# A two-layer trunk on one core: eight feature tiles of each down-projection as seven block products, and V in sixteen parts shifted by a token tile

## The chip, the core and the metric

The kernel runs on one core of a Trainium2 chip. Its parts are TensorE (PE in the profile; it multiplies, into the accumulators of PSUM), VectorE (DVE) and ScalarE (ACT), which read and write PSUM and the on-chip memory, GpSimd (POOL), and the DMA queues, of which SyncE (SP) and GpSimd issue the transfers here. Each engine runs its instructions strictly in the order in which the program has them; an instruction that waits holds everything behind it on its engine. The metric is the device time of one execution in microseconds (us); lower is better.

## The reference

One batch of 512 tokens, width 1024, float32. Layer 0 mixes tokens with differential attention (8 heads, block-causal mask), layer 1 with a gated short convolution. Each is followed by a SwiGLU channel mixer, and each of the four sublayers sits in `x <- LN(alpha * x + sublayer(x))`:

```python
def swiglu(x, w_gate, w_up, w_down):          # D_FF = 2816 = 22 feature tiles of 128
    h = jax.nn.silu(x @ w_gate) * (x @ w_up)
    return h @ w_down
...
for i in range(2):
    m = diff_attention(h, ...) if i == 0 else short_gated_conv(h, ...)
    h = layer_norm(ALPHA * h + m, ln1_g[i], ln1_b[i])
    h = layer_norm(ALPHA * h + swiglu(h, w_gate[i], w_up[i], w_down[i]), ln2_g[i], ln2_b[i])
```

## The kernel before, in words

**Numbers.** Every operand of a large product is split in two rounded parts, hi = round(x) and lo = x - hi, and a product is three matmuls: hi·hi, hi·lo, lo·hi (`mm3`). `split` makes the pair: ScalarE copies hi, VectorE subtracts for lo. Where a weight is used unchanged in gate/up, `plain` makes the pair in another way: ScalarE copies hi, ScalarE copies -hi into lo, and a GpSimd DMA adds the raw weight to lo in place (the accumulate).

**Stages.** Attention (to about 196 us of the profiled execution), the output projection, gate/up of layer 0 (246 to 466), its down-projection (466 to 590), the convolution (590 to 771), gate/up of layer 1 (to 990) and its down-projection (to the end).

**Attention.** For each head h, `project_qk(h)` multiplies q and k in 8 parts and `project_v(h // 2, h % 2)` half of the token tiles of V for a pair of heads in 4 parts: two tiles share a PSUM bank, and one ScalarE copy per bank puts them into `v_sb`. Between these 12 parts, at set places, stand the steps of the head before, `attend(h - 1)`: scores, transposes of the map, and the products with V (`values`, one per query tile `qt`, which reads the tiles 0 to `qt` of `v_sb`).

**Gate/up** is by seven block products (Winograd's form of Strassen's scheme: x11, s2, s1, x12, s3, s4, x22) over 11 units of two feature tiles. The hidden activations of a unit go to a tile `h{u}`, two feature tiles by 512 tokens. The forms of the input lie in slots `f0` to `f13`, named by `HOME`.

**Down-projection** (`project_norm` with name `dn`): 22 feature tiles in 11 groups of two; the output is two halves of 512 columns by four token tiles. For each half, each weight group (one 512 KB load, one `split`) is multiplied with the hidden pairs `hid` of the four token tiles, into one bank per token tile (`o_dn`). Before it, `swiglu` splits the 11 hidden tiles, partly into the slots of the forms. After each half, `residual` adds the bank to `ALPHA *` the residual `res`, and the norm follows.

**Order.** The program has no loop on the chip. A scheduling layer lays the instructions out once, engine by engine, from the order of the code and its own priorities; buffers of a pool rotate, and a load or a write waits until the last reader of its buffer is done.

Of the kernel before, what the change touches and what calls it, by code (L numbers as in the profile page):

```python
# [34 lines left out]
UNITS = KF // 2  # L35
LEAD = 4
# [3 lines left out]
def trunk(ctx: ExitStack, tc: tile.TileContext, t: dict):  # L40
# [208 lines left out]
    def project_norm(lhs, w, kt, gb, xT, out, name, early=None, fetch=None):  # L249
# [10 lines left out]
        def step(ps, wg, gi, j, tt, at=None):  # L260
            k = gi * GROUP + j
            ts = slice(tt * P, (tt + 1) * P)
            n = 512 // len(ps[tt])
            for i in range(len(ps[tt])) if at is None else (at,):
                cs = slice(i * n, (i + 1) * n)
                lh, ll = lhs(k)
                mm3(ps[tt][i][:, :n], (lh[:, ts], ll[:, ts]),
                    (wg[0][:, j, cs], wg[1][:, j, cs]), k == 0, k == kt - 1)

        def residual(ps, hf, tt, i=0):  # L270
            n = 512 // len(ps[tt])
            r = res[:, tt, hf * 512 + i * n : hf * 512 + (i + 1) * n]
            nc.vector.scalar_tensor_tensor(r, r, ALPHA, ps[tt][i][:, :n], op0=ALU.mult, op1=ALU.add)
# [14 lines left out]
        ps = [[bank(f"o_{name}_1_{tt}")] for tt in range(NT)]  # L288
# [33 lines left out]
    with ExitStack() as actx:  # L322
# [111 lines left out]
        def project_v(pair, th):  # L434
            state = {}

            def part(u, half):
                tt = 2 * th + u
                if (u, half) == (0, 0):
                    state["ps"] = bank(f"v_{pair}_{th}")  # L440
                    if pair and th == 0:
# [10 lines left out]
            return [lambda u=u, half=half: part(u, half) for u in range(2) for half in range(2)]  # L452
# [94 lines left out]
        def attend(h):  # L547
# [56 lines left out]
    def swiglu(i, x, turns, open_next, out):  # L604
# [3 lines left out]
        with ExitStack() as fctx:  # L608
# [136 lines left out]
        with ExitStack() as fctx:  # L745
            dx = fctx.enter_context(tc.tile_pool(name=f"dx{i}", bufs=1, reuse_waits="tile"))
            hT = []
            for u in range(UNITS):
                if u == 0:
                    hi = wpool.tile([P, 2, S], F32R, tag="whi", name=f"hid{i}_{u}_hi")  # L750
                    lo = wpool.tile([P, 2, S], F32R, tag="wlo", name=f"hid{i}_{u}_lo")
                elif u < 8:
                    hi, lo = (slot(slots["f"], f"f{2 * u - 2 + j}", (2, S), F32R, f"hid{i}_{u}_{j}") for j in range(2))
                else:
                    hi, lo = (slot(dx, f"d{2 * u + j}", (2, S), F32R, f"hid{i}_{u}_{j}") for j in range(2))
# [125 lines left out]
```

## Time and profile before

| | |
|---|---|
| median of 3 runs (lowest to highest) | 1125.2 us (1124.7 to 1125.24) |
| the profiled execution: its own time, and its span | 1126.72 us, 1124.9 us |
| PE busy | 1105.3 us, 98% of the span |
| VectorE, ScalarE, GpSimd busy | 733.4, 516.8, 115.0 us |
| mean granted clock of PE | 0.997 of full speed |
| bytes moved by DMA | 156.63 MB, mean 139 GB/s |

The span runs from the first to the last instruction that the profiler saw; the execution's own time is 1.8 us longer. Matmuls overlap: the profile gives each its own duration, but the distance between the starts of two that follow each other is what a matmul costs.

### The profile page before, as it was taken

Reading aid. Unit: us, or ns where it says so; the run is one execution under the profiler, and the core shown is the slowest. Engines: PE = TensorE matmul, PEld = TensorE weight load, DVE = VectorE, ACT = ScalarE, POOL = GpSimd, SP = SyncE. Lnnn points to the kernel's source line nnn. Section 1 sums busy time; section 2 is a strip of 40 time slices with the busy share of each in tenths; the row PEclk is TensorE's granted clock in tenths of the full one; section 3 lists DMA queues with packets and bytes.
Section 4 is the critical chain, followed back from the end, with each engine's and each line's share of the span. In section 5 each row is a group of like instructions: output and inputs, shape, how many; then the busy total and the mean of one; then the engine's idle time right before and its main releaser. Section 6 shows DMA issues by size and latency. Waiting matters only on the chain.

```text
span 1124.9 us, 17891 instructions
## 1 busy us (share of the span) xinstructions
PE 1105.3 (98%) x7242; PEld 992.1 (88%) x7242; DVE 733.4 (65%) x1067; ACT 516.8 (46%) x788; POOL 115.0 (10%) x147
## 2 busy tenths in 40 slices
PE   8999999999999999999999999999999999999997
PEld 6878887889999999988889888889999999988886
DVE  7888877588987676924264634448898677672416
ACT  5555555656466566612222323336546556651210
POOL 1111111130011111000010000012001111100002
PEclk9999999999999999999999999999999999999999
DMA  8512132376777875533314433368558777553302
GB/s 276 201 38 76 57 95 75 83 172 200 231 180 205 185 189 133 169 113 92 114 38 137 134 104 95 94 144 214 181 178 205 187 188 180 125 181 94 112 20 75
DMA packets 45027, 156.63 MB, mean 139 GB/s; under 512 B 5232, under 2 KB 6128, under 8 KB 44944
## 3 DMA queue, kind: packets, MB, share of 16 engines
q1 hardware_dynamic: 35728, 121.93, 33.9%
q0 software_dynamic: 9216, 33.56, 16.0%
q8 instruction: 57, 0.93, 0.3%
q14 instruction: 26, 0.21, 0.1%
HBM read 119.81 MB, written 2.10 MB: 108 GB/s over the span
## 4 chain that ended last, share of the span: by engine, by line
PE 85%; DVE 6%; issue 4%; ACT 2%; DMA 2%; POOL 0%; SPq 0%; POOLq 0%; DVEq 0%; ACTq 0%
PE y L636 16%; PE z L636 11%; PE x L636 10%; PE o_dn L75 7%; PE o_dn L76 7%; PE o_dn L74 7%; PE in L74 4%; PE in L76 4%; PE in L75 4%; PE o_wo L74 1%; PE o_wco L74 1%; PE o_wco L76 1%; PE o_wco L75 1%; PE o_wo L76 1%; PE o_wo L75 1%
## 5 line engine op out<-in xcount | busy, mean ns | idle before, releaser
L56 ACT CAST whi_gu_t<-gu_t 128x1024 fp32r<-128x1024 f32 x88 | 89.8, 1049 | 100.5 <-DVE gu_t L624 90.7
L57 DVE TENSOR_TENSOR wlo_dn<-raw_dn,whi_dn 128x1024 fp32r<-128x1024 f32 x44 | 53.3, 1222 | 110.3 <-ACT whi_dn L56 110.3
L74 PE MATMUL o_dn<-whi_dn,hid 128*128 128x512 f32 (+1 forms) x320 | 123.8, 387 | 0.0
L76 PE MATMUL o_dn<-whi_dn,hid 128*128 128x512 f32 (+1 forms) x320 | 123.8, 387 | 0.0
L75 PE MATMUL o_dn<-wlo_dn,hid 128*128 128x512 f32 (+1 forms) x320 | 123.8, 387 | 0.0
L57 DVE TENSOR_TENSOR wlo_gu_t<-gu_t,whi_gu_t 128x1024 fp32r<-128x1024 f32 x88 | 106.3, 1219 | 3.6 <-ACT whi_gu_t L56 3.6
L56 ACT CAST whi_dn<-raw_dn 128x1024 fp32r<-128x1024 f32 x44 | 45.8, 1050 | 135.5 <-PE o_dn L76 106.0
L174 POOL DMA_DIRECT2D wlo_gu<-raw_gu x64 | 55.8, 872 | 432.8 <-ACT wlo_gu L173 377.7
L636 PE MATMUL x<-x_x_hi,whi_gu 128*128 128x256 f32 x352 | 98.6, 280 | 0.0
L636 PE MATMUL x<-x_x_hi,wlo_gu 128*128 128x256 f32 x352 | 98.4, 280 | 0.0
L636 PE MATMUL y<-x_s_hi,wlo_gu_t 128*128 128x256 f32 x352 | 98.3, 279 | 0.0
L636 PE MATMUL y<-x_s_hi,whi_gu_t 128*128 128x256 f32 x352 | 98.3, 279 | 0.0
L636 PE MATMUL x<-x_x_lo,whi_gu 128*128 128x256 f32 x352 | 98.2, 279 | 0.0
L636 PE MATMUL y<-x_s_lo,whi_gu_t 128*128 128x256 f32 x352 | 98.2, 279 | 0.0
L74 PE MATMUL in<-x_hi,whi_in 128*128 128x512 f32 (+1 forms) x240 | 83.7, 349 | 0.0
L76 PE MATMUL in<-x_hi,wlo_in 128*128 128x512 f32 (+1 forms) x240 | 83.2, 347 | 0.0
L75 PE MATMUL in<-x_lo,whi_in 128*128 128x512 f32 (+1 forms) x240 | 82.8, 345 | 0.0
L172 ACT CAST whi_gu<-raw_gu 128x1024 fp32r<-128x1024 f32 x64 | 66.8, 1048 | 30.1 <-PE y L636 21.3
L75 PEld LDWEIGHTS o_dn<-wlo_dn,hid 128*128 128x128 f32 x320 | 60.2, 188 | 13.1
L76 PEld LDWEIGHTS o_dn<-whi_dn,hid 128*128 128x128 f32 x320 | 60.1, 188 | 13.0
L74 PEld LDWEIGHTS o_dn<-whi_dn,hid 128*128 128x128 f32 x320 | 60.2, 188 | 13.0
L173 ACT ACTIVATE wlo_gu<-raw_gu 128x1024 fp32r<-128x1024 f32 x64 | 67.5, 1054 | 7.9 <-PE o_wco L75 6.5
(239 smaller groups left out, 3117.1 us busy)
## 6 DMA issues: line engine op xcount, KB each, us to landing
raw_gu<-in_wgu SPq DMA_DIRECT2D x104, 512.0 KB, 4.6
wlo_gu<-raw_gu POOLq DMA_DIRECT2D x64, 512.0 KB, 5.4
raw_dn<-in_wdn SPq DMA_DIRECT2D x44, 512.0 KB, 3.6
raw_in<-in_win SPq DMA_DIRECT2D x24, 512.0 KB, 3.6
raw_qk<-in_wqk SPq DMA_DIRECT2D x14, 512.0 KB, 3.8
raw_v<-in_wv SPq DMA_DIRECT2D x8, 512.0 KB, 4.8
raw_wo<-in_wo SPq DMA_DIRECT2D x8, 512.0 KB, 3.7
raw_wco<-in_wco SPq DMA_DIRECT2D x8, 512.0 KB, 3.7
```

Of the source, the lines that this page charges most:

```text
L56: nc.scalar.copy(hi, src)
L57: nc.vector.tensor_tensor(lo, src, hi.bitcast(F32), op=ALU.subtract)
L74: nc.tensor.matmul(out, lh, rh, start=first, stop=False)
L75: nc.tensor.matmul(out, lh, rl, start=False, stop=False)
L76: nc.tensor.matmul(out, ll, rh, start=False, stop=last)
L172: nc.scalar.copy(hi, raw)
L173: nc.scalar.activation(lo, raw, AF.Copy, scale=-1.0)
L174: nc.gpsimd.dma_start(lo, raw, accum_op=ALU.add)
L636: nc.tensor.matmul(o, a, b[:, k, :], start=first and f + k + n == 0, stop=k == 3 and n == 2, skip_group_check=True)
```

## The change

In both layers, the feature tiles 0 to 7 of the down-projection (the hidden tiles of units 0 to 3, now one tile `hq`, called `quad`) are multiplied with their 1024 weight rows by seven products of blocks in place of eight. A block is four feature tiles by 256 tokens (`a11`, `a12` of token tiles 0 and 1, even and odd feature tiles; `a21`, `a22` of token tiles 2 and 3), and four feature tiles by 512 columns of the weights (b11, b12, b21, b22; the rows of `wdn` are reordered for this when the inputs are laid out). Each product is 24 matmuls of 512 columns into two banks (x, z or y). Sums of blocks of activations (`v(a11, a11, a21)` and so on, in place) and of weights (t1 to t4) run on VectorE; the sums are split by `split`, the unchanged weight blocks b11, b21 and b22 by `plain`. After a product, VectorE adds its banks to the quarters of `res` that need it, while later products go on accumulating in the same banks. The other 14 feature tiles are multiplied as before, into the banks x, y and z as they stand.

V is projected in sixteen parts, one token tile of a pair of heads each, with a bank and a ScalarE copy of 256 columns each; head 0 has three of them, the heads 1 to 6 two, head 7 one, so that each stands one tile earlier. The products with V stand at the places 6, 7, 9 and 11 for every head.

```diff
 CHUNK = 4
...
     def fetch_gu(i):
         lead[i] = []
+        more = slot(slots["xb"], "hq", (4, 4, 256), F32R, f"wlead{i}")
...
+            pair = (more[:, 2 * u - 4], more[:, 2 * u - 3]) if u >= 2 else None
...
         def residual(ps, hf, tt, i=0):
...
+            if carry is not None and (hf or tt >= 2):
+                nc.vector.tensor_tensor(r, r, ps[tt][i][:, :n], op=ALU.add)
+            else:
+                nc.vector.scalar_tensor_tensor(r, r, ALPHA, ps[tt][i][:, :n], op0=ALU.mult, op1=ALU.add)
...
-        ps = [[bank(f"o_{name}_0_{tt}")] for tt in range(NT)]
+        ps = carry[:4] if carry is not None else [[bank(f"o_{name}_0_{tt}")] for tt in range(NT)]
...
-        def project_v(pair, th):
+        def project_v(pair, tt):
...
-                if (u, half) == (1, 1):
-                    nc.scalar.copy(v_sb[:, 2 * th : 2 * th + 2, pair * 256 : (pair + 1) * 256],
-                                   ps.rearrange("p (t e) -> p t e", t=2))
+                if half == 1:
+                    nc.scalar.copy(v_sb[:, tt, pair * 256 : (pair + 1) * 256], ps[:, :256])
...
-            for qt, i in zip(range(NT), (6, 7, 11, 12) if h % 2 == 0 else (6, 7, 9, 11)):
+            for qt, i in zip(range(NT), (6, 7, 9, 11)):
                 steps[i].append(lambda qt=qt: values(h, qt))
...
             parts = project_qk(h)
-            parts += project_v(h // 2, h % 2)
+            for n in range(2 * h + 1 if h else 0, min(2 * h + 3, 16)):
+                parts += project_v(n // NT, n % NT)
...
+            def load(a, b, g, pool, tag, n):
+                raw = pool.tile([P, 2, 512], F32, tag=tag, name=f"raw_dn{i}_{a}{b}_{g}", bufs=n)
+                nc.sync.dma_start(raw, t["wdn"][i][:, b, CHUNK * a + 2 * g : CHUNK * a + 2 * g + 2, :])
+                return raw
...
+            def plain_dn(raws, name):
+                return [plain(raw, "", pair_dn(f"{name}_{g}")) for g, raw in enumerate(raws)]
+
+            def combined_dn(raws, name):
+                out = []
+                for g, raw in enumerate(raws):
+                    out.append(pair_dn(f"{name}_{g}"))
+                    split(*out[-1], raw)
+                return out
...
+            def product(ps, key, w, first):
+                hi, lo = left[key]
+                for u in range(CHUNK):
+                    wh, wl = w[u // 2]
+                    for j in range(2):
+                        ts = slice(j * P, (j + 1) * P)
+                        mm3(ps[j], (hi[:, u, ts], lo[:, u, ts]), (wh[:, u % 2, :], wl[:, u % 2, :]),
+                            first and u == 0, u == CHUNK - 1, skip_group_check=True)
...
+            banks = {n: [bank(f"{n}_dn{i}_{j}") for j in range(2)] for n in "xzy"}
+            b11 = [load(0, 0, g, wpool, "raw", 3) for g in range(2)]
+            w = plain_dn(b11, "11")
+            form("x11", a11)
+            product(banks["x"], "x11", w, True)
+            b12 = [load(0, 1, g, dx, "b12", 2) for g in range(2)]
+            t1 = sums_dn(b11, b12, b11)
+            form("x12", a12)
+            v(a11, a11, a21, op=ALU.subtract)
+            v(a21, a21, a22, op=ALU.add)
+            form("s1", a21)
+            product(banks["z"], "s1", combined_dn(t1, "t1"), True)
+            for th, half in ((1, 1), (0, 1), (1, 0)):
+                add(th, half, banks["x"], ALPHA)
+            b22 = [load(1, 1, g, dx, "b22", 2) for g in range(2)]
+            t2 = sums_dn([dx.tile([P, 2, 512], F32, tag="t2", name=f"t2_dn{i}_{g}", bufs=2) for g in range(2)], b22, t1)
+            form("x22", a22)
+            v(a22, a22, a11, op=ALU.subtract)
+            form("s2", a22)
+            halve("x11")
+            product(banks["y"], "s2", combined_dn(t2, "t2"), True)
+            add(1, 1, banks["z"])
+            b21 = [load(1, 0, g, dx, "b21", 2) for g in range(2)]
+            halve("s1")
+            product(banks["x"], "x12", plain_dn(b21, "21"), False)
+            add(0, 1, banks["y"])
+            form("s3", a11)
+            halve("s2")
+            t3 = sums_dn(b12, b22, b12)
+            product(banks["y"], "s3", combined_dn(t3, "t3"), False)
+            v(a12, a12, a22, op=ALU.subtract)
+            form("s4", a12)
+            halve("x12")
+            product(banks["z"], "s4", plain_dn(b22, "22"), False)
+            add(1, 1, banks["y"])
+            t4 = sums_dn(t2, b21, t2)
+            halve("s3")
+            product(banks["y"], "x22", combined_dn(t4, "t4"), False)
+            halve("s4")
+            halve("x22")
```

`form(key, src)` splits a block of activations into the slots `HOME[key]`; `halve(key)` splits the hidden tile of the next of units 4 to 10 into the same slots, once the product that read them is done; `add` adds two banks to a quarter of `res` (the three with `ALPHA` by one multiply-and-add).

**How the order of instructions moves.** The rows below are instructions of the built programs in the order of one engine: line, operation, output <- inputs, shape of the output. The lines of the rows after the change are those of the changed kernel, 1 to 110 higher.

The first place is VectorE in layer 0, from the last gate/up unit's `c210_10` on (the first instruction there that reads the last gate/up product). Before the change, the rest of the unit stands between splits of hidden tiles (`hid0_*`) and of weights (`wlo_dn0_*`) for the plain down-projection:

```order
L697 TENSOR_TENSOR c210_10_5521<-e0_10_5329,y0_10_5340 128x512
L57 TENSOR_TENSOR wlo_dn0_0_2_5656<-raw_dn0_0_2_5653,whi_dn0_0_2_5655 128x1024
L57 TENSOR_TENSOR hid0_1_1_5534<-h0_1_3510,hid0_1_0_5533 128x1024
L699 TENSOR_TENSOR h0_10_5490<-c210_10_5521,w50_10_5396 128x2x256
L57 TENSOR_TENSOR wlo_dn0_0_3_5686<-raw_dn0_0_3_5683,whi_dn0_0_3_5685 128x1024
L57 TENSOR_TENSOR wlo_dn0_0_4_5716<-raw_dn0_0_4_5713,whi_dn0_0_4_5715 128x1024
L57 TENSOR_TENSOR hid0_8_1_5562<-h0_8_5022,hid0_8_0_5561 128x1024
```

After the change:

```order
L704 TENSOR_TENSOR c210_10_5531<-e0_10_5339,y0_10_5350 128x512
L58 TENSOR_TENSOR dn0_x22_lo_5650<-hq0_3352,dn0_x22_hi_5649 128x1024
L706 TENSOR_TENSOR h0_10_5500<-c210_10_5531,w50_10_5406 128x2x256
L840 TENSOR_TENSOR hq0_3352<-hq0_3352 128x4x256
L853 TENSOR_TENSOR hq0_3352<-hq0_3352 128x4x256
L809 SCALAR_TENSOR_TENSOR res_88<-res_88,x_dn0_0_5539 128x512
L809 SCALAR_TENSOR_TENSOR res_88<-res_88,x_dn0_1_5540 128x512
L791 TENSOR_TENSOR raw_dn0_00_0_5545<-raw_dn0_01_0_5587,raw_dn0_00_0_5545 128x1024
L809 SCALAR_TENSOR_TENSOR res_88<-res_88,x_dn0_0_5539 128x512
L791 TENSOR_TENSOR raw_dn0_00_1_5547<-raw_dn0_01_1_5589,raw_dn0_00_1_5547 128x1024
L58 TENSOR_TENSOR wlo_dn0_t1_0_5604<-raw_dn0_00_0_5545,whi_dn0_t1_0_5603 128x1024
L809 SCALAR_TENSOR_TENSOR res_88<-res_88,x_dn0_1_5540 128x512
```

Behind `c210_10` there now stand the lo part of x22, the last hidden tile, the two in-place sums of activations (L840, L853) and two adds of the first product's banks, and only then the two sums t1 (written over `raw_dn0_00`), with an add between them; `wlo_dn0_t1_0`, which the second product needs, comes tenth behind `c210_10`. Behind it follow an add, `wlo_dn0_t1_1`, two adds, the two sums t2, the lo of s2, the lo of `hid0_4`, and `wlo_dn0_t2_0`.

The second place is the third and fourth product (y = s2·t2, x = x12·b21) on TensorE, after the change; before it, nothing of the kind stood there:

```order
L75 MATMUL y_dn0_0_5543<-whi_dn0_t2_0_5662,dn0_s2_hi_5654 128x512
L75 MATMUL y_dn0_1_5544<-whi_dn0_t2_0_5662,dn0_s2_hi_5654 128x512
L75 MATMUL x_dn0_0_5539<-whi_dn0_21_0_5704,dn0_x12_hi_5593 128x512
L75 MATMUL x_dn0_1_5540<-whi_dn0_21_0_5704,dn0_x12_hi_5593 128x512
L76 MATMUL y_dn0_0_5543<-wlo_dn0_t2_0_5663,dn0_s2_hi_5654 128x512
L77 MATMUL y_dn0_0_5543<-whi_dn0_t2_0_5662,dn0_s2_lo_5655 128x512
L76 MATMUL y_dn0_1_5544<-wlo_dn0_t2_0_5663,dn0_s2_hi_5654 128x512
```

The first four are hi·hi matmuls of both products; the other 22 of y stand behind the first two of x. On ScalarE, the copies for the same products stand like this after the change (`whi` and `wlo` of 21 are made by `plain`, of t2 by `split`):

```order
L57 CAST whi_dn0_t2_0_5662<-t2_dn0_0_5645 128x1024
L57 CAST hid0_5_hi_5700<-h0_5_4330 128x1024
L57 CAST whi_dn0_t2_1_5666<-t2_dn0_1_5646 128x1024
L173 CAST whi_dn0_21_0_5704<-raw_dn0_10_0_5696 128x1024
L173 CAST whi_dn0_21_1_5709<-raw_dn0_10_1_5698 128x1024
L174 ACTIVATE wlo_dn0_21_0_5705<-raw_dn0_10_0_5696 128x1024
```

A little later on ScalarE, the copies for the sixth product (z = s4·b22) have the hi of `hid0_7` in front of their second half; it is written into the slots of x12, which the fourth product reads:

```order
L173 CAST whi_dn0_22_0_5791<-raw_dn0_11_0_5641 128x1024
L173 CAST whi_dn0_22_1_5796<-raw_dn0_11_1_5643 128x1024
L57 CAST hid0_7_hi_5787<-h0_7_4798 128x1024
L174 ACTIVATE wlo_dn0_22_0_5792<-raw_dn0_11_0_5641 128x1024
L174 ACTIVATE wlo_dn0_22_1_5797<-raw_dn0_11_1_5643 128x1024
```

The accumulate DMA that completes `wlo_dn0_22_0` stands on GpSimd behind the fourth of these.

The third place is TensorE at the end of head 1's parts, where `values(0, ...)` multiplies with V. Before the change, the products with the token tiles 2 and 3 (`aTs_0_2`, `aTs_0_3`) stand among the first matmuls of the next head's k, right behind the last part of V:

```order
L76 MATMUL v_0_1_503<-whi_v0_1_165,x0_lo_93 128x256
L516 MATMUL o_0_0_476<-v_sb_103,aTs_0_2_499 128x128 x2
L74 MATMUL k_2_591<-x0_hi_92,whi_qk2_0_581 128x512
L75 MATMUL k_2_591<-x0_lo_93,whi_qk2_0_581 128x512
L76 MATMUL k_2_591<-x0_hi_92,wlo_qk2_0_582 128x512
L74 MATMUL k_2_591<-x0_hi_92,whi_qk2_0_581 128x512
L516 MATMUL o_0_0_476<-v_sb_103,aTs_0_2_499 128x128
L516 MATMUL o_0_0_476<-v_sb_103,aTs_0_3_545 128x128 x4
```

After it, the product for query tile 3 stands behind a whole part of the next pair's V (24 matmuls `v_1_0` of 256 columns, of which the last three are shown):

```order
L75 MATMUL v_1_0_560<-whi_v1_1_569,x0_hi_92 128x256
L76 MATMUL v_1_0_560<-wlo_v1_1_570,x0_hi_92 128x256
L77 MATMUL v_1_0_560<-whi_v1_1_569,x0_lo_93 128x256
L517 MATMUL o_0_0_504<-v_sb_103,aTs_0_3_590 128x128 x4
L75 MATMUL k_2_633<-x0_hi_92,whi_qk2_0_623 128x512
```

The same holds for heads 2 and 4. For head 6 no further part of V is left: there the last part, `v_3_3`, stands directly ahead of the product that reads it.

## Rows read from the trace of the kernel before

**Rows 1.** The page, parts 1 and 4: engines, and the chain that ended last.
```profile
PE 1105.3 (98%) x7242; PEld 992.1 (88%) x7242; DVE 733.4 (65%) x1067; ACT 516.8 (46%) x788; POOL 115.0 (10%) x147
...
PE 85%; DVE 6%; issue 4%; ACT 2%; DMA 2%; POOL 0%; SPq 0%; POOLq 0%; DVEq 0%; ACTq 0%
```

**Rows 2.** What PE waited for: us in total, times, longest us.
```profile
PE z L636 <- DMA wlo_gu<-raw_gu: 3.4, 2, 2.5
PE o L516 <- ACT v_sb L449: 3.4, 4, 0.9
```

**Rows 3.** Chain of waits around layer 0's gate/up end: start us, us, what.
```profile
443.86 2.83 PE y L636 x24
...
463.65 2.83 PE y L636 x24
466.48 0.23 PE o_dn L74
```

**Rows 4.** Busy us (x instructions) of PE, PEld, DVE, ACT, POOL in a stretch; PEclk; DMA.
```profile
466.00:511.00 45.00, 45.00 (x198) 36.42 (x197) 18.45 (x18) 12.87 (x14) 0.00 (x0) 1.00 0.45 140
```

**Rows 5.** VectorE in order of time: start us, us, instruction [idle before <-releaser].
```profile
446.73 0.69 DVE L697 TENSOR_TENSOR c<-e,y 128x512 f32<-128x512 f32 x1 [0.27 <-PE y L636]
...
451.12 1.23 DVE L57 TENSOR_TENSOR hid<-h,hid 128x1024 fp32r<-128x1024 f32 x1 [2.16 <-ACT hid L56]
...
452.99 1.22 DVE L624 TENSOR_TENSOR gu_t<-raw_gu,gu_t 128x1024 f32<-128x1024 f32 x1
...
461.53 0.68 DVE L685 TENSOR_TENSOR w<-w,y 128x512 f32<-128x512 f32 x1
462.13 2.35 DVE L57 TENSOR_TENSOR hid<-h,hid 128x1024 fp32r<-128x1024 f32 x2
...
91.45 1.98 DVE L57 TENSOR_TENSOR wlo_v<-raw_v,whi_v 128x1024 fp32r<-128x1024 f32 x1
```

**Rows 6.** ScalarE in order of time, the same stretch.
```profile
448.14 1.04 ACT L173 ACTIVATE wlo_gu<-raw_gu 128x1024 fp32r<-128x1024 f32 x1
...
450.04 1.05 ACT L56 CAST hid<-h 128x1024 fp32r<-128x1024 f32 x1
...
454.29 1.05 ACT L56 CAST whi_gu_t<-gu_t 128x1024 fp32r<-128x1024 f32 x1 [0.86 <-DVE gu_t L624]
...
457.15 1.99 ACT L56 CAST whi_dn<-raw_dn 128x1024 fp32r<-128x1024 f32 x2
```

**Rows 7.** GpSimd in order of time; DMA to landing in 425 to 500 us.
```profile
449.54 0.87 POOL L174 DMA_DIRECT2D wlo_gu<-raw_gu  x1 [5.29 <-ACT wlo_gu L173]
...
raw_dn<-in_wdn SPq DMA_DIRECT2D x13, 512.0 KB, 3.7
wlo_gu<-raw_gu POOLq DMA_DIRECT2D x4, 512.0 KB, 5.0
...
DMA to landing us min/median/max: 4.5/5.0/5.9
```

**Rows 8.** Attention, PE and ScalarE in order of time, around a head's end.
```profile
46.13 0.61 PE L516 MATMUL o<-v_sb,aTs 128*128 128x128 f32 x4
...
48.39 1.38 PE L516 MATMUL o<-v_sb,aTs 128*128 128x128 f32 x10 [0.72 <-ACT v_sb L449]
46.81 1.05 ACT L56 CAST whi_qk<-raw_qk 128x1024 fp32r<-128x1024 f32 x1 [1.21 <-DMA raw_qk<-in_wqk]
47.76 0.58 ACT L449 COPY v_sb<-v 128x512 f32<-128x512 f32 x1
```

**Rows 9.** Chain at gate/up's start in both layers, and the stretch behind (as rows 4).
```profile
279.88 2.86 PE z L636 x22
...
800.44 5.91 DMA wlo_gu<-raw_gu
...
806.39 4.39 PE z L636 x22
...
807.00:812.00 5.00, 5.00 (x32) 5.00 (x31) 1.73 (x3) 2.62 (x3) 0.85 (x1) 0.67 0.87 286
```

More of the change, by code (lines that the diff above doesn't have):

```diff
@@ L70, in weights, with mm3 @@
         return hi, lo
-    def mm3(out, lhs, rhs, first, last):
+    def mm3(out, lhs, rhs, first, last, **kw):
         (lh, ll), (rh, rl) = lhs, rhs
-        nc.tensor.matmul(out, lh, rh, start=first, stop=False)
-        nc.tensor.matmul(out, lh, rl, start=False, stop=False)
-        nc.tensor.matmul(out, ll, rh, start=False, stop=last)
+        nc.tensor.matmul(out, lh, rh, start=first, stop=False, **kw)
+        nc.tensor.matmul(out, lh, rl, start=False, stop=False, **kw)
+        nc.tensor.matmul(out, ll, rh, start=False, stop=last, **kw)
     warm = const.tile([P, 512], mybir.dt.bfloat16, name="warm")
@@ L287, in project_norm @@
             residual(ps, 0, tt)
-        ps = [[bank(f"o_{name}_1_{tt}")] for tt in range(NT)]
+        ps = carry[4:] if carry is not None else []
+        ps = ps + [[bank(f"o_{name}_1_{tt}")] for tt in range(len(ps), NT)]
         if out is not None:
@@ L431, in project_qk, with part @@
             return [lambda i=i, kp=kp: part(i, kp) for i, kp in order]
-        def project_v(pair, th):
+        def project_v(pair, tt):
             state = {}
[L437 to L441, printed above, removed]
+            def part(half):
+                if half == 0:
+                    state["ps"] = bank(f"v_{pair}_{tt}")
+                    if pair and tt == 0:
                         heads[pair, "w"] = v_weights(pair)
@@ L746, in swiglu @@
             dx = fctx.enter_context(tc.tile_pool(name=f"dx{i}", bufs=1, reuse_waits="tile"))
-            hT = []
[L748 to L755, printed above, removed]
+            v = nc.vector.tensor_tensor
@@ new lines, in swiglu, with form @@
+            quad = hid["quad"]
+            a11, a12, a21, a22 = (
+                quad[:, :, f, th * HALF : (th + 1) * HALF] for th in range(2) for f in range(2)
+            )
+            left = {}
+            def form(key, src):
+                hi, lo = left[key] = tuple(
+                    slot(slots["f"], f"f{f}", (CHUNK, HALF), F32R, f"dn{i}_{key}_{p}")
+                    for f, p in zip(HOME[key], ("hi", "lo"))
+                )
+                split(hi, lo, src)
+            def load(a, b, g, pool, tag, n):
+                raw = pool.tile([P, 2, 512], F32, tag=tag, name=f"raw_dn{i}_{a}{b}_{g}", bufs=n)
+                nc.sync.dma_start(raw, t["wdn"][i][:, b, CHUNK * a + 2 * g : CHUNK * a + 2 * g + 2, :])
+                return raw
@@ new lines, in add, with halve @@
+            def add(th, half, ps, factor=None):
+                for j in range(2):
+                    r = res[:, 2 * th + j, half * 512 : (half + 1) * 512]
+                    if factor is None:
+                        v(r, r, ps[j], op=ALU.add)
+                    else:
+                        nc.vector.scalar_tensor_tensor(r, r, factor, ps[j], op0=ALU.mult, op1=ALU.add)
+            hT = []
+            def halve(key):
+                u = CHUNK + len(hT)
+                hi, lo = (
+                    slot(slots["f"], f"f{f}", (2, S), F32R, f"hid{i}_{u}_{p}")
+                    for f, p in zip(HOME[key], ("hi", "lo"))
+                )
@@ L849, in halves, with by_halves @@
         return w.reshape(-1, P, 2, 512).transpose(1, 2, 0, 3)
+    def by_halves(w):
+        order = [*range(0, 2 * CHUNK, 2), *range(1, 2 * CHUNK, 2), *range(2 * CHUNK, KF)]
+        return w.reshape(KF, P, D)[order].reshape(DFF, D)
     qkv = a["attn_w_qkv"][0]
@@ L866 @@
         "wgu": gu.transpose(0, 5, 1, 2, 4, 3, 6),
-        "wdn": np.stack([halves(a["ffn_w_down"][i]) for i in range(2)]),
+        "wdn": np.stack([halves(by_halves(a["ffn_w_down"][i])) for i in range(2)]),
         "ln1_g": a["ln1_g"], "ln1_b": a["ln1_b"], "ln2_g": a["ln2_g"], "ln2_b": a["ln2_b"],
```

36 lines of the change are left out of this document (22 added, 14 removed).

## The prediction

> **What bounds the kernel now.** I read the page first: PE is busy 98% of the span and is 85% of the chain that ended last [rows 1]. Then the waits of PE: two groups of 3.4 us each are all that matters, one at the start of gate/up, one in attention [rows 2]. Then the chain around the end of layer 0's gate/up: its products follow each other every 2.83 us (24 matmuls of 256 columns, 0.118 us each), and the down-projection's matmuls follow without a gap [rows 3]. There 198 matmuls of 512 columns fill 45.0 us: 0.227 us each [rows 4]. So a matmul taken away is time gained, and any wait put in front of PE is time lost. VectorE, ScalarE and the DMA queues cost nothing now; the question is whether the new work stays hidden.
>
> **What is taken away.** In each layer 8 tiles x 4 token tiles x 2 halves x 3 = 192 matmuls become 7 x 24 = 168. By 0.227 us that is 43.6 against 38.1 us, 5.45 us a layer. In the last layer the last token tile's 24 matmuls were pairs of 256 columns (2 x 0.118 against 0.227): another 0.2 us.
>
> **Prices of the new work.** A VectorE instruction on 1024 elements lasts 1.22 us and lets the next start after 1.13 (two last 2.35); one on 512, half from PSUM, lets it start after 0.60 (461.53 to 462.13) [rows 5]. ScalarE's copy of 1024 lasts 1.05, the next starts after 0.94 (two last 1.99) [rows 6]. Hand-overs: PE to VectorE 0.04 (446.73 after 443.86 + 2.83) [rows 3, 5]; ScalarE to VectorE 0.03 (451.12 after 450.04 + 1.05); VectorE to ScalarE 0.08 (454.29 after 452.99 + 1.22); ScalarE to GpSimd 0.36 (449.54 after 448.14 + 1.04) [rows 5 to 7]. To PE I take 0.04, as from the DMA (806.39 after 800.44 + 5.91) [rows 9]. An accumulate lands 5.0 us after its issue there, 4.5 to 5.9 [rows 7]. The in-place sums over a strided block do not occur before: bounds are 0.60 (half the elements) and 1.98, the slowest of this size [rows 5]; I take 1.13, as they have the same count and type.
>
> **The seven products, step by step.** Time 0 is the end of gate/up's last product; VectorE and ScalarE follow the order shown for the changed kernel.
>
> First product, x11·b11: its forms and weights are made during the last unit, it runs 0 to 5.45. Second, s1·t1: VectorE does `c210_10` from 0.04. The lo of x22 needs ScalarE's hi, which writes into the slot that the last gate/up product read: 0.04 + 1.05, so it starts at 1.12. Then the hidden tile at 2.25, the two in-place sums at 2.85 and 3.98, two adds at 5.11 and 5.71, and t1's first half from 6.31 to 7.53; ScalarE's hi ends at 8.66. PE starts at 8.70: **it waits 3.25**. It has two hi·hi matmuls, to 9.15, then needs the lo: an add, t1's second half, and `wlo_dn0_t1_0` from 9.17 to 10.39: **1.3 more**. The other 22 matmuls end at 15.4. The loads of b12 are no part of this: they go out when `c210_10` frees the gate/up buffers, and land some 3.7 us later [rows 7], near 4.5.
>
> Third, s2·t2: VectorE goes on at 10.30 with an add (0.60), a split (1.13), two adds, t2's first half from 13.23 to 14.45, its second at 14.36, the lo of s2 at 15.49, that of `hid0_4` at 16.62, `wlo_dn0_t2_0` from 17.75 to 18.97. ScalarE's hi of t2 ends at 15.58, so PE waits 0.2 and has two matmuls, to 16.1. Next on PE stand two of x12·b21, whose hi is the fourth copy on ScalarE from 14.53 on: it ends at 18.40, **a wait of 2.35**. Those two end at 18.9, the lo of t2 is there at 19.0, the 22 end at 24.0. Fourth, x12·b21: ScalarE copies -hi from 19.23 to 20.28, the accumulate is issued at 20.64 and lands at 25.64: **1.7**. The 22 end at 30.7. Fifth, s3·t3: its operands are ready near 29.9 (each product's adds wait for its end, the splits behind them follow at once): no wait, to 36.1. Sixth, s4·b22: its -hi stands on ScalarE behind the hi of `hid0_7`, which waits until the fourth product has read x12, 30.7. So 30.74, copy from 31.7 to 32.75, issue at 33.1, landing at 38.1; PE has done one matmul by 36.35: **1.8**. 23 matmuls to 43.4, and the seventh, whose sums are long ready, to 48.8.
>
> The waits are 10.7 us, twice what the 24 matmuls give. The stretch takes 48.8 against 43.6: **+5.2 us a layer**, +10.4 for both, as the order in layer 1 is the same. The splits of the other hidden tiles go into slots that come free by product, and the last 14 tiles have 5.45 us of PE for 1.13 us of VectorE in each group: hidden.
>
> **V.** Of PE's 3.4 us for `v_sb`, one wait stands in each of four head ends, 0.7 to 0.9. In one the copy starts 1.6 us after PE's last V matmul, behind a weight copy that waits for its load, and ends at 48.34, 2.2 us after it [rows 8]. Now 24 matmuls of 256 columns (2.8 us) stand in between at three of the four; at the last nothing does. That takes off 3 x 0.86 = 2.6 us; bounds 1.5 (something else is late next, such as the next weights) and 3.4. ScalarE's eight further small copies are hidden, as it waits there itself.
>
> **The sum.** +10.4 - 0.2 - 2.6 = **+7.6 us**: 1126.7 of the profiled execution becomes 1134.3. The median shown is 1.5 lower than that execution; I keep that distance: **1132.8 us**, 0.7% slower. Bounds: accumulates at 4.5 and 5.9 move it by -2.0 and +3.6, V by -0.8 and +1.1, in-place sums at 1.98 by +3.4 at most: 1130 to 1140.9 with everything at its worst.
>
> **Rivals.** *The low clock.* In layer 1 PE waited 2.5 us for an accumulate, and 22 matmuls then took 4.39 us in place of 2.6; the granted clock was 0.67 in that stretch, a mixture of 2.4 and 1.2 GHz. In layer 0 a wait of 0.9 was followed by 2.86 for the same 22 [rows 2, 9]. So a low stretch costs 1.8. Behind the first wait it is swallowed by the 2.35 that PE waits next. If it followed each of the later waits too, the third product's 1.8 would be swallowed by the 1.7, the fourth's moves the sixth's copies (+1.8), and the sixth's adds 1.8: +3.7 a layer, 1140.2 us. The Trainium skill (TensorE: Matmul & The Clock Gate, "HAM oscillation — how this bites in real kernels") describes such a kernel: a wait before each short group of matmuls, and each group begins at the low clock. The trace shows it after one wait and not after the other; that the later waits are shorter than 2.5 speaks against it here.
>
> *It comes to nothing.* If the accumulates landed like plain loads, 3.7 us [rows 7], as the DMA engines have less to do there than in gate/up, 1.3 us goes from each of four waits: +2.4, and with all of V's 3.4 us +1.6: 1126.8 us. Against it: the quickest accumulate took 4.5.
>
> *Faster: the sums of the weights are off PE's path.* The first waits all hang on VectorE between `c210_10` and `wlo_dn0_t2_0`. Were t1 ready at 5.45 and t2 at 10.9, as the weights are before, where PE goes over without a gap [rows 3], 3.5 us of waits would be left: (3.5 - 5.45) x 2 - 2.8 = -6.7, 1118.5 us. It decides from waits under 5.5 a layer on. For it: the weights need nothing from gate/up. Against it: t1 stands behind two adds that cannot start before the first product's end, and behind a load into buffers that gate/up holds.
>
> **How the numbers follow.** My forecast 0.66, the low clock 0.14, nothing 0.11, faster 0.09. About 0.2%, 2.25 us, is what a measurement of this kernel tells from no change. Slower holds the first two, 0.80; same 0.11; faster 0.09. The range reaches down through a part of "nothing" and up to the low clock: 1127 to 1140; the forecast's own is 1129 to 1138.
>
> **What would show it.** Per layer, PE waiting for ScalarE before the second product and again before the x12·b21 pair, for VectorE's `wlo` of t1, and for two accumulates, near 3.3, 2.4, 1.3, 1.7 and 1.8 us; 336 instead of 384 matmuls for these tiles; the three waits for `v_sb` gone and the one of head 6 left; the clock lowered behind the first wait at most. A second product that starts less than 2 us after the first, or waits of less than 5.5 us in all in a layer, would make the prediction wrong.

## The result, and the profile after

The changed kernel takes **1134.2 us** (1134.0 to 1135.2 over 4 runs) against 1125.1 (1124.7 to 1125.2): ratio 1.0085, 95% interval [1.007, 1.01]. It is slower, as forecast; 1132.8 was forecast, 1127 to 1140 the range. Its profiled execution took 1134.0 us, with a span of 1132.2.

The page of the changed kernel, parts 1 and 4 (for [rows 1]):
```profile
PE 1100.7 (97%) x7170; PEld 984.1 (87%) x7170; DVE 783.1 (69%) x1121; ACT 548.9 (48%) x826; POOL 125.1 (11%) x159
...
PE 88%; issue 4%; DVE 3%; DMA 3%; ACT 1%; SPq 0%; POOL 0%; POOLq 0%; DVEq 0%; ACTq 0%
```
72 matmuls were taken away, 24 of 512 columns in layer 0 and 48 of 256 in layer 1, 11.1 us at 0.227 and 0.118, yet PE's busy time went down by only 4.6: other matmuls became slower. What PE waited for (for [rows 2]; us in total, times, longest):
```profile
PE z_dn L75 <- ACT whi_dn_t L57: 6.4, 2, 3.2
PE x_dn L75 <- ACT whi_dn L173: 4.8, 2, 2.4
PE z L639 <- DMA wlo_gu<-raw_gu: 2.9, 2, 1.6
PE z_dn L76 <- DVE wlo_dn_t L58: 2.1, 2, 1.1
PE z_dn L76 <- DMA wlo_dn<-raw_dn: 1.9, 2, 1.0
...
PE o L517 <- ACT v_sb L451: 1.1, 1, 1.1
```
Four waits are new, each once a layer, and three of the four waits for `v_sb` are gone. PE in order of time in layer 0 (start us, us, instruction, [idle before <-releaser]; the first piece is the last matmul of x11·b11, the others begin a product or go on with one):
```profile
466.67 0.40 PE L77 MATMUL x_dn<-whi_dn,dn_x_lo 128*128 128x512 f32 x1
470.27 0.74 PE L75 MATMUL z_dn<-whi_dn_t,dn_s_hi 128*128 128x512 f32 x2 [3.21 <-ACT whi_dn_t L57]
472.06 0.79 PE L76 MATMUL z_dn<-wlo_dn_t,dn_s_hi 128*128 128x512 f32 x1 [1.06 <-DVE wlo_dn_t L58]
...
478.81 0.63 PE L75 MATMUL y_dn<-whi_dn_t,dn_s_hi 128*128 128x512 f32 x2
481.82 0.89 PE L75 MATMUL x_dn<-whi_dn,dn_x_hi 128*128 128x512 f32 x2 [2.38 <-ACT whi_dn L173]
482.51 0.63 PE L76 MATMUL y_dn<-wlo_dn_t,dn_s_hi 128*128 128x512 f32 x1
...
489.07 0.44 PE L76 MATMUL x_dn<-wlo_dn,dn_x_hi 128*128 128x512 f32 x1
```
From 470.27 to 478.81 PE has 24 matmuls and 1.06 us of waiting; at 0.2333 us each that would be 6.66 us together, and it takes 8.54. From 478.81 to 489.07 it has 26 matmuls and 2.38 us of waiting: 10.26 us where 8.45 were due. The windows over the same stretch (columns as in [rows 4]; the granted clock is the third number from the end) show why: 0.57 behind the two long waits, a mixture of 2.4 and 1.2 GHz.
```profile
467.00:472.00 5.00, 0.80 (x3) 0.30 (x2) 5.00 (x7) 4.00 (x4) 0.00 (x0) 1.00 1.03 415
472.00:476.00 4.00, 3.94 (x10) 3.14 (x11) 4.00 (x7) 0.00 (x0) 0.00 (x0) 0.57 0.59 209
476.00:479.00 3.00, 3.00 (x14) 2.44 (x13) 3.00 (x4) 1.23 (x2) 0.00 (x0) 1.00 0.55 167
479.00:482.00 3.00, 0.62 (x3) 0.18 (x2) 2.76 (x4) 3.00 (x4) 0.00 (x0) 1.00 0.59 186
482.00:486.00 4.00, 4.00 (x11) 3.14 (x12) 3.54 (x5) 2.71 (x4) 1.72 (x2) 0.57 0.17 33
```
Where the 7.3 us of span went, between landmarks on PE. "Down" is from the first matmul of the down-projection to the first of the next projection (`in`, 590.19 before, 592.40 after).

| stretch | before | after | difference |
|---|---|---|---|
| to gate/up of layer 0 (attention) | 245.83 | 240.99 | -4.8 |
| gate/up, layer 0 | 220.48 | 220.31 | -0.2 |
| down, layer 0 | 123.88 | 131.10 | +7.2 |
| gate/up, layer 1 (771.30 to 994.36; 773.51 to 994.16) | 223.06 | 220.65 | -2.4 |
| down, layer 1, and the end | 130.5 | 138.0 | +7.5 |

### The profile page after: what moved, and what is told of

The parts are those of the page before. It is cut to its first block, busy times and chain, and to the rows that moved or that the text cites. A ratio compares the mean times of both kernels' runs of the same rounds, so it can differ in the third digit from the quotient of the medians.

```text
span 1132.2 us, 17895 instructions
## 1 busy us (share of the span) xinstructions
PE 1100.7 (97%) x7170; PEld 984.1 (87%) x7170; DVE 783.1 (69%) x1121; ACT 548.9 (48%) x826; POOL 125.1 (11%) x159
## 4 chain that ended last, share of the span: by engine, by line
PE 88%; issue 4%; DVE 3%; DMA 3%; ACT 1%; SPq 0%; POOL 0%; POOLq 0%; DVEq 0%; ACTq 0%
PE y L639 15%; PE z L639 10%; PE x L639 10%; PE in L75 4%; PE in L77 4%; PE in L76 4%; PE z_dn L76 2%; PE z_dn L77 2%; PE y_dn L76 2%; PE z_dn L75 2%; PE y_dn L77 2%; PE y_dn L75 2%; PE o L517 1%; PE o_wo L75 1%; PE x_dn L75 1%
## 5 line engine op out<-in xcount | busy, mean ns | idle before, releaser
L639 PE MATMUL x<-x_x_hi,whi_gu 128*128 128x256 f32 x320 | 89.4, 279 | 0.0
L639 PE MATMUL x<-x_x_hi,wlo_gu 128*128 128x256 f32 x320 | 89.2, 279 | 0.0
L58 DVE TENSOR_TENSOR wlo_dn<-raw_dn,whi_dn 128x1024 fp32r<-128x1024 f32 x28 | 34.1, 1223 | 57.2 <-ACT whi_dn L57 57.1
L57 ACT CAST whi_dn<-raw_dn 128x1024 fp32r<-128x1024 f32 x28 | 29.2, 1050 | 77.5 <-PE y_dn L77 61.0
L639 PEld LDWEIGHTS y<-x_s_hi,wlo_gu_t 128*128 128x128 f32 x352 | 66.1, 188 | 0.0
L639 PEld LDWEIGHTS y<-x_s_lo,whi_gu_t 128*128 128x128 f32 x352 | 66.0, 188 | 0.0
L639 PEld LDWEIGHTS y<-x_s_hi,whi_gu_t 128*128 128x128 f32 x352 | 66.0, 187 | 0.0
L639 PEld LDWEIGHTS x<-x_x_hi,wlo_gu 128*128 128x128 f32 x320 | 60.1, 188 | 0.0
L639 PEld LDWEIGHTS x<-x_x_lo,whi_gu 128*128 128x128 f32 x320 | 60.0, 188 | 0.1
L639 PEld LDWEIGHTS x<-x_x_hi,whi_gu 128*128 128x128 f32 x320 | 60.0, 188 | 0.1
```

What stands on the lines that cost most here:

```text
L57: nc.scalar.copy(hi, src)
L58: nc.vector.tensor_tensor(lo, src, hi.bitcast(F32), op=ALU.subtract)
L639: nc.tensor.matmul(o, a, b[:, k, :], start=first and f + k + n == 0, stop=k == 3 and n == 2, skip_group_check=True)
```

## The experiments

Ratios are to the kernel before on the same chip: 1123.7 us for `e1` to `e4`, 1123.5 for `e5` to `e8` (nine runs from 1121.4 to 1125.0, a tenth 1116.2), 1123.0 for `e9` to `e11`. Each kernel is the changed one with the edit shown, unless said. "Down" is that of layer 0 in the profile.

**The two parts alone.** `e1_v_alone` is the kernel before with only the V part of the diff, `e2_blocks_alone` the changed kernel with that part (`project_v`, the places in `attend`, the parts of a head) put back.

> The kernel before with V in sixteen parts alone. By the prediction's step: three of four waits for v_sb gone, -2.6 us, 1122.5 us. By the two traces: attention and output projection became 4.8 us shorter in the changed kernel, and gate/up of layer 1 2.4 us shorter (its wait for the accumulate 1.6 in place of 2.5 us, and no slow stretch behind it). If the first is all V's doing and the second is not, 1120.3 us; if both are, 1117.9 us. The rival is that V's gain needs the other part: no change, 1125.1 us.

> The changed kernel with V as before, in eight parts. By the prediction's step: +10.4 -0.2 us, 1135.3 us. By the two traces: the down-projection of layer 0 takes 131.1 us in place of 123.9 and that of layer 1 6.7 us more, which gives 1139.0 us if the shorter gate/up of layer 1 comes from V, and 1136.6 us if it comes from the block products' side.

V alone: 1119.3 us, 0.9961 [0.9947, 0.9974], which is -4.4 us. Blocks alone: 1139.4 us, 1.0142 [1.0128, 1.0156], which is +15.7; its down is 131.68. The waits for `v_sb`, with blocks alone and with V alone:
```profile
PE o L519 <- ACT v_sb L452: 3.4, 4, 0.9
```
```profile
PE o L514 <- ACT v_sb L448: 1.2, 1, 1.2
```
V is worth 4.4 us, not 2.6. 2.2 us of it are these waits, as the prediction argued. Gate/up begins at 240.23 us with V alone and at 245.02 with blocks alone, 4.8 apart; 0.6 more of that is one wait of PE for `p`, which is also gone with V, and the last 2.0 stand in no wait that the trace lists: open. The 2.4 us of layer 1's gate/up come, in the profiles, with the blocks: that stretch is 222.5 us with V alone (765.30 to 987.80) and 221.0 with blocks alone (778.25 to 999.21), against 223.06 before. The time of the blocks alone fits this less well: 1139.4 us is nearer to the 1139.0 expected if these 2.4 us were V's than to 1136.6.

**Keeping PE busy through the long waits.** Constant matmuls into a spare bank, 14 behind the first product and 11 behind the second; their result is not used.
```diff
-            product(banks["x"], "x11", w, True)
+            end = product(banks["x"], "x11", w, True)
+            spare = bank(f"spare{i}")
+            filler(end, 14)
...
-            product(banks["z"], "s1", combined_dn(t1, "t1"), True)
+            end = product(banks["z"], "s1", combined_dn(t1, "t1"), True)
+            filler(end, 11)
```


> The changed kernel with 14 matmuls of a constant tile into an unused bank behind the first product and 11 behind the second, in each layer; their result is used by nothing. Theory 1, the clock falls because PE stands still: the 22 matmuls of the second product take 5.1 us in place of 6.75, the copies that wait for the second product's end start that much earlier, the granted clock of that stretch is 1.00, and the third product's 22 are faster too: 3 us a layer, 1128 us. Theory 2, these matmuls are slow for another reason, such as the six loads that land at the same time: they stay at 6.75 us, and the time stays at 1134 us or rises by what the added matmuls delay.

1131.4 us, 1.0074 [1.0062, 1.0087]; down 129.56. Windows and one wait of this kernel:
```profile
467.00:472.00 5.00, 4.45 (x19) 1.77 (x18) 5.00 (x7) 3.77 (x5) 0.00 (x0) 1.00 1.03 419
472.00:476.00 4.00, 3.33 (x14) 2.74 (x15) 4.00 (x6) 0.56 (x1) 0.00 (x0) 1.00 0.76 271
...
482.00:486.00 4.00, 4.00 (x19) 3.23 (x18) 3.82 (x5) 1.73 (x2) 1.72 (x2) 1.00 0.45 89
```
```profile
PE x_dn L76 <- DMA wlo_dn<-raw_dn: 2.0, 2, 1.1
```
The clock is 1.00 where it was 0.57, and z's last 22 matmuls take 5.24 us (472.67 to 477.91) in place of 6.75. The DMA engines were as full as before (1.03, 419 GB/s): contention as the reason falls. But only 1.5 us a layer came back: x12's accumulate, which the low clock had covered, is now waited for, 1.1 us.

**The hidden tiles' splits behind the weights.** On ScalarE the copies for `hid_5` and `hid_7` come after the weights that the next product needs.
```diff
-            halve("s1")
-            product(banks["x"], "x12", plain_dn(b21, "21"), False)
+            w21 = plain_dn(b21, "21")
+            with tc.issue_after(made["ACT"].ins):
+                halve("s1")
+            product(banks["x"], "x12", w21, False)
...
-            halve("x12")
-            product(banks["z"], "s4", plain_dn(b22, "22"), False)
+            w22 = plain_dn(b22, "22")
+            with tc.issue_after(made["ACT"].ins):
+                halve("x12")
+            product(banks["z"], "s4", w22, False)
```


> The changed kernel with the splits of two hidden tiles put behind the weights of the x12 and the s4 product on ScalarE; nothing else. Theory 1, the hi copy of hid_5, which waits for the second product's end, holds up the copies behind it: the wait of 2.4 us in front of x12's pair falls by 0.9 to 1.0 us, and the wait for the accumulate of 22 (0.94) goes; with what then waits for VectorE's lo of t2, 0.8 to 1.5 us a layer less, 1131.2 to 1132.6 us. Rival: the wait passes whole to VectorE's lo of t2, which stands right behind, and nothing is gained, 1134.2 us.

1127.9 us, 1.0043 [1.0031, 1.0056]; down 127.94, 3.2 less, more than either theory had. The row of 2.4 us is gone from the list of waits, 0.26 for the lo of t2 is left in its place (0.56 in layer 1), and with the wait the low clock behind it has gone:
```profile
479.00:482.00 3.00, 2.74 (x12) 1.93 (x11) 3.00 (x4) 3.00 (x5) 0.59 (x1) 1.00 0.62 179
482.00:486.00 4.00, 3.92 (x17) 2.82 (x15) 3.80 (x6) 2.28 (x4) 1.13 (x2) 1.00 0.87 164
```
So this wait costs its own 2.4 us and the 1.8 behind it. A part is taken back: in layer 0 by the 0.26 and by a second product that is 0.5 us slower in this profile, in layer 1 by the 0.56 and by 0.93 for b21's accumulate.

**b22 without the accumulate.** Its lo comes from VectorE (`combined_dn(b22, "22")` for `plain_dn`).

> The changed kernel with b22 split by ScalarE and VectorE in place of ScalarE twice and an accumulate. The wait of 0.94 us for the accumulate in front of the sixth product goes, if VectorE has its two lo parts done by then: 1 us a layer, 1132 us. Rival: VectorE's two more instructions hold up the sums t4 and with them the seventh product, and PE waits there: the same 1134 us.

A single run: 1130.7 us, down 130.18, 0.9 less. The wait of 1.0 for this accumulate is gone, and PE has no new wait for VectorE.

**The loads early.** b12 and b22 are put into buffers that gate/up has left by then, so that their loads go out during its last units; the order on the engines stays.

> The changed kernel with the loads of b12 and b22 alone moved ahead of gate/up's end; the order on VectorE and ScalarE is as in the changed kernel. If the first wait is VectorE's order (t1 behind two sums and two adds), it stays at 3.2 us, and the time at 1134 us. If it is the load that lands late, the sum t1 starts earlier, and the wait falls to 2 us or less.

A single run: 1144.8 us, down 136.88. The waits:
```profile
PE x_dn L76 <- DMA wlo_dn<-raw_dn: 6.2, 3, 3.1
PE z_dn L75 <- ACT whi_dn_t L57: 6.0, 2, 3.0
```
The wait in front of the second product stays at 3.0, as it should if the order on VectorE makes it. But the time does not stay at 1134: b11's accumulate is now late, by 3.1 us in layer 0 and 2.2 in layer 1 (the third of these waits, 1.0, is for b21's), which no theory had foreseen.

**The sums of the weights first.** VectorE makes t1 and its lo ahead of the adds, then s2, t2, the adds and t3; ScalarE makes the weights ahead of the hidden tiles' splits; the early loads are needed for it. The diff, cut to its core:
```diff
+            b12 = [load(0, 1, g, dx, "b12", 2) for g in range(2)]
+            b22 = [load(1, 1, g, dx, "b22", 2) for g in range(2)]
             w = plain_dn(b11, "11")
...
-            product(banks["z"], "s1", combined_dn(t1, "t1"), True)
-            for th, half in ((1, 1), (0, 1), (1, 0)):
-                add(th, half, banks["x"], ALPHA)
...
+            form("s3", a11)
+            t1 = sums_dn(b11, b12, b11)
+            w_t1 = combined_dn(t1[:1], "t1a")
+            behind = made["DVE"]
+            w_t1 += combined_dn(t1[1:], "t1b")
+            product(banks["z"], "s1", w_t1, True)
+            with tc.issue_after(behind.ins):
+                a22_made = v(a11, a22, a11, op=ALU.subtract)
+                form("s2", a11)
...
+            with tc.issue_after(a22_made.ins):
+                t2 = sums_dn(t2_out, b22, t1)
...
+            with tc.issue_after(dv.ins):
+                for th, half in ((1, 1), (0, 1), (1, 0)):
+                    add(th, half, banks["x"], ALPHA)
+                t3 = sums_dn(b12, b22, b12)
...
+                for key in ("x11", "s1", "s2", "x12"):
+                    halve(key)
```


> The seven products as in the changed kernel and in the same order on TensorE, with the work around them in another order: the loads of b12 and b22 go out before gate/up's end (they lie where gate/up's earlier buffers were), VectorE makes t1 and t2 ahead of the adds, s2 is written over a11 so that x22's lo can come later, ScalarE makes the weights ahead of the hidden tiles, and the last three hidden tiles are made by ScalarE and an accumulate. If the loss of the changed kernel is the four waits and the clock that two of them cost, nearly all of it goes: one wait of 1.3 us for the lo of t2 is left in a layer, at full clock, 504 matmuls by 0.233 and the rest of the stretch as before give 121.4 us where the changed kernel takes 131.1: 1134.2 - 19.4 = 1114.8 us, ratio to the kernel before 0.991. Rival: VectorE is the bound of this stretch (it is busy over nine tenths of it), so its work passes behind the seven products and PE waits there: no more than half of it comes back, 1124 us or more.

1117.6 us, 0.9946 [0.9932, 0.9959]; down 123.45. All four new waits are gone. One has come, inside the first product; the waits, the DMA issues of 455 to 500 us (count, KB each, median us to landing) and the window behind it:
```profile
PE x_dn L78 <- DMA wlo_dn<-raw_dn: 4.7, 2, 2.6
```
```profile
wlo_dn<-raw_dn POOLq DMA_DIRECT2D x2, 512.0 KB, 10.8
```
```profile
465.00:468.00 3.00, 2.95 (x7) 2.37 (x8) 1.22 (x1) 1.04 (x1) 0.00 (x0) 0.52 0.98 274
```
b11's two accumulates land 10.5 and 11.2 us after their issue, while the early loads are under way; in the changed kernel the same two took 5.2 and 6.3, and accumulates took 5.0 in [rows 7]. With the loads early alone they take 11.0, which is the 3.1 there.

**Four hidden pairs elsewhere.** As the last, but the split hidden tiles of x11, s1, s2 and x22 lie in the weight blocks' buffers instead of the slots of the forms.

> The same, with four of the seven split hidden tiles in the free buffers of the weight blocks in place of the slots of the forms. In the kernel before, matmuls whose hidden tile lay in a form's slot followed each other every 0.233 us, and those whose hidden tile lay elsewhere every 0.227. If it is the place that decides, 4 x 48 matmuls a layer go from 0.233 to 0.227: 1.3 us a layer, 2.6 us less than the reordered kernel. If it is something else (which matmuls stand side by side, or the transfers of that time), they stay at 0.233, and the time is the same.

1117.1 us, 0.9944 [0.9931, 0.9956]; down 122.97. Its matmuls on these tiles follow each other every 0.2267 us, the others every 0.2333; the gain in time is within the interval, as the accumulate's wait grew to 2.9.

**b11 without the accumulate.** In both of the last kernels `plain_dn(b11, "11")` becomes `combined_dn(b11, "11")` (`e9_split11_low`, `e10_split11`), and so in the one with the early loads alone (`e11_early_split11`).

> As the reordered kernel with four of seven hidden pairs in the weight blocks' buffers, but b11 comes as the half-sum's two parts by ScalarE and VectorE in place of the accumulating transfer. Theory (the wait of 2.9 us a layer there is that transfer sharing the DMA engines with the early loads): no wait on that transfer in the first product, the first product's matmuls at 0.227 to 0.233 without a low clock, a wait of about 1.3 us a layer left for the second sum's low part; the down stretch 122.97 to about 119 to 120, the time 1117.1 to about 1110 (1108 to 1113). Rival (VectorE is full there, and its two more instructions of 0.6 us each delay the first half-sum): a wait of 1 to 2.5 us in front of the second product takes the place, the time 1114 to 1117.

> The same without the low slots: b11 split on ScalarE and VectorE, all hidden pairs where they lay in the changed kernel. Theory: the wait on the accumulating transfer (2.6 us a layer) and the slow stretch behind it (about 1.6) go; 1117.6 to about 1111 (1109 to 1114). Against the kernel of the same call with low slots: 0.5 to 1 us a layer slower by the pitch (120 matmuls by 0.0067 us is 0.8). Rival: a wait for the first half-sum takes its place, 1115 to 1118.

> The kernel with the two early loads in the changed kernel's own order, but b11 by ScalarE and VectorE in place of the accumulating transfer. Theory (the 3.1 us waits there come from the accumulating transfer beside the early loads): those waits go, the first wait of 3 us for the first half-sum stays or grows by up to 1.2 us since VectorE has two more instructions ahead of it, time about 1144.8 less 6 to 12 = 1133 to 1139. Rival (the early loads delay the plain loads themselves, whatever the accumulate): waits for the loaded blocks remain, 1142 or more.

With the four hidden pairs elsewhere (`e9_split11_low`): **1111.2 us, 0.9896 [0.9881, 0.9911]**, down 119.54; with all of them in the slots (`e10_split11`): 1112.7 us, 0.9909 [0.9893, 0.9926], down 120.63. Early loads alone, a single run: 1135.0 us, down 132.08, its wait in front of the second product 3.2. The wait for b11's accumulate is gone in all three, so the conflict is between it and the loads. VectorE's two more instructions (next start after 1.13 each, not 0.6) brought no wait in front of the second product; 0.95 for the lo of t2 is left in the third, near the 1.3 that was expected. The early loads by themselves gain nothing: what t1 waits for is the order. Waits of the first of them, and pieces of its PE on both sides of the change of place (six matmuls from one row to the next within each pair):
```profile
PE z L641 <- DMA wlo_gu<-raw_gu: 2.1, 2, 1.2
PE y_dn L78 <- DVE wlo_dn_t L60: 1.9, 2, 1.0
```
```profile
513.09 0.39 PE L77 MATMUL x_dn<-whi_dn,hid_hi 128*128 128x512 f32 x1
514.45 0.39 PE L77 MATMUL y_dn<-whi_dn,hid_hi 128*128 128x512 f32 x1
...
522.73 0.40 PE L77 MATMUL y_dn<-whi_dn,hid_hi 128*128 128x512 f32 x1
524.13 0.40 PE L77 MATMUL x_dn<-whi_dn,hid_hi 128*128 128x512 f32 x1
```
1.36 us against 1.40 for six: 0.2267 and 0.2333 each. In `e10_split11` the first pair too takes 1.40 (513.38 to 514.78).

## Why the prediction was right, and where its steps were not

The direction was right for the reason given: the products' operands pass through VectorE and ScalarE in an order that makes PE wait longer than the 24 matmuls take. The last reordered kernels show that the order is the reason: with the same products their down takes 119.5 and 120.6 us, 4.3 and 3.3 less than before, where `e11_early_split11`, with the same early loads and the same split of b11 in the changed kernel's order, takes 132.1. The total came out within 1.4 us by luck, as errors cancelled. Per layer, from layer 0:

| term | forecast | measured |
|---|---|---|
| 24 matmuls less | -5.45 | -4.2 |
| hi of t1, before the second product | 3.25 | 3.21 |
| lo of t1 | 1.3 | 1.06 |
| t2 | 0.2 | 0 |
| -hi and hi of b21, behind `hid_5` | 2.35 | 2.38 |
| accumulate of b21 | 1.7 | 0 |
| accumulate of b22 | 1.8 | 0.9 |
| low clock behind the waits | 0 | 1.9 + 1.8 |
| sum | +5.2 | +7.2 (terms: 7.1) |

The waits were 7.6 us in place of the 10.7 forecast, and 3.7 of low clock, put at nothing, came in place of the rest.

**The first three waits** were walked instruction by instruction along VectorE and ScalarE, and came out within 0.25 us.

**"Behind the first wait it is swallowed by the 2.35 that PE waits next": this step failed.** The 2.35 is no fixed appointment. ScalarE in order of time, changed kernel:
```profile
478.83 1.05 ACT L57 CAST hid_hi<-h 128x1024 fp32r<-128x1024 f32 x1 [1.67 <-PE z_dn L76]
479.78 1.04 ACT L57 CAST whi_dn_t<-t_dn 128x1024 fp32r<-128x1024 f32 x1
480.72 1.99 ACT L173 CAST whi_dn<-raw_dn 128x1024 fp32r<-128x1024 f32 x2
```
The copy for `hid_5` waits for the end of the second product, and b21's copies stand behind it. A second product at the low clock ends 1.9 us later and pushes the wait along whole. That the wait itself came out at 2.38 is luck in part: the walk had the four copies follow each other without a pause, with `hid_5` free just in time, where in the run ScalarE stood idle for 1.67 us first. The sign "the clock lowered behind the first wait at most" failed too: it was also lowered behind the 2.38. The rival of the low clock was priced at 3.7 us a layer, and 3.7 is what it cost, but by another sum: 1.9 behind the first waits and 1.8 behind the 2.38, none behind the accumulates; with 0.14 it had too small a chance. Its rule (the Trainium skill, TensorE: Matmul & The Clock Gate, "HAM oscillation — how this bites in real kernels": groups of matmuls with a wait ahead of each begin at the low clock) agrees with the trace behind the waits of 3.21 and 2.38 us, 0.57 granted, and with the filled kernel, 1.00; behind the 0.94 in front of the sixth product the clock stayed at 1.00.

The same wait of 2.38 did not always lower the clock. In `e11_early_split11` the matmuls behind it follow each other every 0.233 us, 21 steps from 483.92 to 488.82:
```profile
483.35 0.73 PE L75 MATMUL x_dn<-whi_dn,dn_x_hi 128*128 128x512 f32 x2 [2.38 <-ACT whi_dn L173]
483.92 0.39 PE L76 MATMUL y_dn<-wlo_dn_t,dn_s_hi 128*128 128x512 f32 x1
...
488.82 0.40 PE L77 MATMUL y_dn<-whi_dn_t,dn_s_lo 128*128 128x512 f32 x1
```
What decides between the two stays open.

**The accumulates** were mis-sized, 3.5 us a layer for 0.9. b21's was covered by the third product's low clock, as the rival had said: filling the waits brought 1.1 us of it back. b22's is not covered so, as it stands behind the copy for `hid_7`, which waits for the fourth product's end. It came to 0.94 because it was issued 0.1 us sooner behind that end than forecast, landed after 4.56 us in place of 5.0 (496.58 to 501.14), and PE was busy 0.3 us longer ahead of it; taking it away gained 0.9.

**The 24 matmuls** were priced at 0.227, from [rows 4]. That was a misreading: five of the 198 matmuls there are the last of gate/up, of 256 columns; the others start every 0.2327 us (192 steps from 466.31 to 510.98). And the pace differs by hidden tile. Windows of 30 us in the kernel before, hidden tiles 1 to 6 and then from tile 8 on, and one of the changed kernel:
```profile
472.00:502.00 30.00, 30.00 (x130) 24.18 (x129) 10.94 (x10) 6.30 (x6) 0.00 (x0) 1.00 0.48 156
512.00:542.00 30.00, 30.00 (x133) 24.64 (x132) 13.33 (x15) 6.44 (x7) 0.00 (x0) 1.00 0.37 107
```
```profile
512.00:542.00 30.00, 30.00 (x130) 24.18 (x129) 8.86 (x8) 7.34 (x7) 0.00 (x0) 1.00 0.44 137
```
In the kernel before, the tiles 1 to 7 run at 0.2333 us a matmul and 0, 8, 9 and 10 near 0.2267; the changed kernel has the lower count throughout. So 24 times 0.2333, 5.6 us, are saved, and up to 192 times 0.0067, 1.3 us, lost. In `e10_split11`, down less its one wait is 120.63 - 0.95 = 119.7, 4.2 us under before (the row of the table); in `e9_split11_low`, with four tiles moved, 119.54 - 0.95 = 118.6, 5.3 under.

**V** was mis-sized: 2.6 forecast, 4.4 measured (2.9 to 6.0 by the interval).

**Layer 1's gate/up** was not in the sum. Its wait had been 2.5 us, and 22 matmuls at the low clock behind it took 4.39 [rows 9]. In the chain of waits after, the accumulate lands after 5.11 us instead of 5.91, the wait is 1.6, and the clock stays:
```profile
802.57 5.11 DMA wlo_gu<-raw_gu
...
807.73 2.86 PE z L639 x22
```
It seems to come with the blocks: in the eleven profiles of kernels that have them this wait is 0.9 to 1.8 us and the clock stays, in the two without, 2.5 and 2.0, it falls. What makes that transfer quicker was not tried.

Together, in the spans: the two down stretches grew by 14.7 us where 10.2 was forecast, and the rest fell by 7.4 where 2.6 was forecast, so that +7.3 met the +7.6. The rival "faster" (waits under 5.5 us a layer, 1118.5 us) names its condition rightly: the reordered kernels meet it, with 2.1 to 2.9 and then 1.0 to 1.2 us of waits a layer.

## What to carry to other kernels

A wait on PE of the length seen here, 2 to 3 us, is to be priced with the low clock that may follow, and with what it pushes: before a delay is called "swallowed by the next wait", look whether the next wait hangs on the end of the delayed work. Saving matmuls by sums of operands paid here only once those sums, and the weights' splits, stood ahead of everything on VectorE and ScalarE that PE doesn't need next. A load moved earlier has to be weighed against the transfers that it then shares the DMA engines with.

## What the runs showed of the hardware

- A matmul of 512 columns took 0.2267 or 0.2333 us at a granted clock of 1.00, by the buffer in which its stationary tile lies: the same tiles changed their pace when they were moved (1.36 to 1.40 us for six). Why one place is quicker stays open.
- An accumulating transfer of 512 KB took 5.0 us to land in [rows 7]; b11's two took 5.2 and 6.3 in the changed kernel, and 10.5 and 11.2 beside the early loads.
- Behind the 14 waits of PE of 2.9 to 3.2 us in all profiles here the granted clock fell (changed kernel: 0.57 over 4 us). Behind 16 waits of 2.0 to 2.6 us it fell 13 times (0.52 over 3 us behind 2.56; with V alone 0.72 over 6 us behind 2.0) and stayed at 1.00 three times (twice behind 2.38, once behind 2.61). Behind single waits of 0.9 to 1.8 us it stayed at 1.00. Constant matmuls in the wait kept it at 1.00.
